# A row-wise softmax with relative-position bias: the last row of the first chunk in 16 small transfers on ScalarE's queue

## The chip, the cores and the metric

The kernel runs on one core of a Trainium2 chip. The metric is the device time of one execution in microseconds, lower is better. A core has VectorE (DVE), ScalarE (ACT), GpSimd (POOL), TensorE (PE, not used here) and SyncE (SP), and 16 DMA engines that move data between the chip's memory (HBM) and the on-chip memory of 128 partitions. DMAs are issued by SP and ACT, each on a queue of its own; in the profile SP's is q1 and ACT's is q10. The 16 engines serve both queues.

## The reference

```python
B, H, S, max_rel = 2, 8, 2112, 16
rel = pos[:, None] - pos[None, :]
rel_clipped = np.clip(rel, -max_rel, max_rel) + max_rel
logits = logits + rel_bias[:, rel_clipped][None]
logits = logits - logits.max(axis=-1, keepdims=True)
exp = np.exp(logits)
return exp / exp.sum(axis=-1, keepdims=True)
```

The logits are 2 x 8 x 2112 x 2112 in float32, 285 MB; as much is written. The bias has 33 values per head, chosen by the clipped distance of row and column.

## The kernel before, in words

**Tiles.** A row of scores has S = 2112 elements, 8448 B. W = 33 consecutive rows go to one partition, and 64 such groups make one head; the 128 partitions hold two heads. A round k (K = 4 of them, L202) handles two heads of both batch entries. Within a round the 33 rows of a partition are cut into chunks of 6, 5, 6, 5, 6, 5 rows (SIZES), for b = 0 and b = 1, so a round has NT = 12 chunks, and a row of a partition lies contiguous in memory, as do a chunk's rows. There are four buffers X[0] to X[3] (NBUF); chunk m uses X[m % 4], with a semaphore `ld` for its load and `st` for its store.

**Bias strip.** The tile F holds the bias as a strip of 2112 + 32 values per partition; row i of a partition adds the strip shifted by i. F is built from rel_bias once per round by `strip(k)` (L143 to L158) on DVE. Before the first round, rel_bias itself is loaded into the start of F by one DMA on ACT's queue (L107), over four partitions, after DVE has zeroed that part (L105); DVE waits for it at L133 (semaphore `rb`), spreads it by a shuffle (L134) and copies it into place (L140).

**Compute of a chunk.** `add(m)` on DVE takes the load's semaphore and, for each row, adds the strip, negates and finds the minimum (L173). `exps(m)` on ACT takes each row as it comes and does the exponential with its sum (L181). `scale(m)` on DVE takes all of a chunk's exponentials, forms the reciprocals (L189) and scales the first DV = 3 rows (L193); `scale_rest(m)` on ACT scales the others (L198). DVE's order in a round is strip, then add(0), scale(0), add(1), scale(1) and so on; ACT's is exps(0), scale_rest(0), exps(1) and so on.

**Transfers.** SP issues all loads (L88) and stores (L96). First the four loads of chunks 0 to 3, one after another without a wait; then store(0); then for each next chunk n: store n, wait until store n - 1 has landed, and load chunk n + 3 into the buffer so freed (`turn`, L215 to L219). `take` (L83) waits for a semaphore to reach a value and takes that off again. The last chunk's store is cut into two, its first three rows and the rest.

A transfer over 128 partitions with n rows of chunk m has this shape of addresses, one contiguous run per partition:

```python
ap=[[W * S, P], [1, n * S]]
```

Of the kernel before, what the change touches and what calls it, by code (L numbers as in the profile page):

```python
# [15 lines left out]
def kernel(  # L16
# [6 lines left out]
    nc = tc.nc  # L23
    P = 128
    B, H, S, S2 = logits.shape
    assert S == S2
    MR = 16
    W = 2 * MR + 1
# [5 lines left out]
    NBUF = 4  # L34
    SIZES = [6, 5, 6, 5, 6, 5]
# [8 lines left out]
    X = [io.tile([P, R * S], FP32, tag=f"X{b}", name=f"X{b}") for b in range(NBUF)]  # L44
# [11 lines left out]
    def view(t, offset, dims):  # L56
        return bass.AP(tensor=t.tensor, offset=t.offset + offset, ap=[[list(t.ap[0])[0], P]] + dims)

    def rows(t, k, m, s0, n):

        b, j, r = CH[m]
        return bass.AP(
            tensor=t.tensor,
            offset=t.offset + (b * H * S + j + s0) * S + k * (2 * S * S),
            ap=[[W * S, P], [1, n * S]],
        )

    with tc.tile_critical(no_gpsimd_drain=True):  # L68
        ld = [nc.alloc_semaphore(f"ld{b}") for b in range(NBUF)]
        st = [nc.alloc_semaphore(f"st{b}") for b in range(NBUF)]  # L70
        added = nc.alloc_semaphore("added")
        expd = nc.alloc_semaphore("expd")
# [13 lines left out]
        def load(k, m):  # L86
            b, r = m % NBUF, CH[m][2]
            nc.sync.dma_start(out=X[b][:, 0 : r * S], in_=rows(logits, k, m, 0, r)).then_inc(ld[b], 16)  # L88
# [8 lines left out]
                out=rows(out, k, m, s0, n), in_=X[b][:, s0 * S : (s0 + n) * S]  # L97
            ).then_inc(st[b], 16)

        for m in range(NBUF):  # L100
            load(0, m)

        Q = 32
        step = list(F.ap[0])[0]
# [3 lines left out]
            out=bass.AP(tensor=F.tensor, offset=F.offset, ap=[[Q * step, P // Q], [1, H * W]]),  # L108
            in_=bass.AP(tensor=rel_bias.tensor, offset=rel_bias.offset, ap=[[0, P // Q], [1, H * W]]),
# [7 lines left out]
        v = nc.vector  # L117
        done = [0]

        def then(ins):  # L120
            done[0] += 1
            ins.then_inc(dve, 1)

        def settle():
            take(v, dve, done[0])
            done[0] = 0
# [9 lines left out]
        for h in range(2):  # L136
            p = slice(h * NB, (h + 1) * NB)
            src = bass.AP(tensor=F.tensor, offset=F[p].offset + h * W,
                          ap=[[list(F.ap[0])[0], NB], [2 * W, K], [1, W]])
# [3 lines left out]
        def strip(k):  # L143

            then(v.tensor_copy(out=rbK[:, :], in_=rbP[:, bass.ds(k, 1), :]))  # L145
            settle()
            low, high = rbK[:, W - 1 : W], rbK[:, 0:1]
            blocks = view(F, MR, [[W, NB], [1, W]])
            then(v.tensor_tensor(out=blocks, in0=view(eq, 0, [[1, NB], [0, W]]),  # L149
                                 in1=view(rbK, W - 1, [[0, NB], [-1, W]]), op=ALU.mult))  # L150
            then(v.tensor_scalar(out=rest, in0=lt, scalar1=low, scalar2=None, op0=ALU.mult))  # L151
            then(v.tensor_copy(out=F[:, 0:MR], in_=low.to_broadcast([P, MR])))  # L152
            then(v.tensor_copy(out=F[:, FW - MR : FW], in_=high.to_broadcast([P, MR])))  # L153
            settle()
            then(v.scalar_tensor_tensor(out=rest, in0=gt, scalar=high, in1=rest, op0=ALU.mult, op1=ALU.add))  # L155
            settle()
            then(v.tensor_tensor(out=blocks, in0=blocks, in1=view(rest, 0, [[1, NB], [0, W]]), op=ALU.add))  # L157
            settle()  # L158
# [10 lines left out]
        def add(m):  # L169
            take(v, ld[m % NBUF], 16)  # L170
            j, r = CH[m][1:]
            for i in range(r):
                v.tensor_tensor_reduce(  # L173
                    out=row(m, i), in0=row(m, i), in1=F[:, W - 1 - j - i : W - 1 - j - i + S],
                    scale=-1.0, scalar=BIG, op0=ALU.add, op1=ALU.min, accum_out=col(nmax, m, i),
                ).then_inc(added, 1)
# [9 lines left out]
        def scale(m):  # L186
            r = CH[m][2]
            take(v, expd, r)
            v.reciprocal(out=col(rec, m, 0, r), in_=col(tot, m, 0, r)).then_inc(inv, 1)  # L189
            v.wait_ge(inv, 1).then_inc(inv, -1)  # L190
            v.sem_inc(invA, 1)
            for i in range(DV):
                v.tensor_scalar_mul(out=row(m, i), in0=row(m, i), scalar1=col(rec, m, i)).then_inc(scaled, 1)  # L193
# [7 lines left out]

        with nc.Fori(0, K, 1, engines=[ENG.DVE]) as k:  # L202
            strip(k)
            for m in range(NT):
                add(m)
                scale(m)
# [54 lines left out]
```

## Time and profile before

| what | value |
|---|---|
| time, median of 3 runs | 1329.12 us (1329.1 to 1329.44) |
| the profiled execution's own time | 1329.3 us |
| its span, from first to last instruction | 1327.5 us |
| moved | 571.00 MB, half read and half written |
| DVE, ACT busy | 819.7 us, 808.8 us |

In a line of the timeline the numbers are the start and the length in us, then the engine, the line of the code and the operation; "SPq" and "ACTq" are the queues of instructions of SP and ACT that issue DMAs, and an "x4" merges four issues into the stretch from the first's start to the last's end. A bracket gives the idle time of the engine before the instruction and what ended it. "DMA to landing" is the time from an issue to the completion of its transfer.

### The profile page before, as it was taken

To read this page: it belongs to the slowest core of one execution; us is meant where nothing else is said; L and a number is where in the kernel's file an instruction comes from. 1 tells how busy PE (TensorE), PEld (TensorE's weight loads), DVE (VectorE), ACT (ScalarE), POOL (GpSimd) and SP (SyncE) were. 2 spreads that over 40 slices of the span, in tenths; PEclk is the share of its full clock that TensorE was granted. 3 is DMA by queue.
4 is the path that set the end of the run, shared out by engine and by line. 5 is a ranking of instruction groups with operands and counts; after the bars stand their busy time and mean duration, and the time that the engine had idled before them with its cause. 6 is when DMAs were issued, how large, how long until landed. Compare 5 with 4: busy or idle time off the path is not lost. (4 is left out here: it accounts for less than half of the span.)

```text
span 1327.5 us, 2383 instructions
## 1 busy us (share of the span) xinstructions
DVE 819.7 (62%) x756; ACT 808.8 (61%) x652; POOL 0.6 (0%) x6
## 2 busy tenths in 40 slices
DVE  6875665558655566556866466664686547665572
ACT  3885575655756557555676566764667646675472
POOL 0000000000000000000000000000000000000000
DMA  9999999999999999999999999999999999999998
GB/s 407 427 424 425 430 433 429 432 431 433 434 430 438 423 439 431 432 432 433 438 436 429 433 430 435 433 430 441 427 439 428 435 431 437 434 436 427 436 427 376
DMA packets 13981, 571.00 MB, mean 430 GB/s; under 512 B 1556, under 2 KB 1560, under 8 KB 1560
## 3 DMA queue, kind: packets, MB, share of 16 engines
q1 hardware_dynamic: 13968, 570.96, 99.8%
q14 instruction: 5, 0.04, 0.0%
q10 hardware_dynamic: 8, 0.00, 0.0%
HBM read 285.48 MB, written 285.47 MB: 430 GB/s over the span
## 5 line engine op out<-in xcount | busy, mean ns | idle before, releaser
L173 DVE CUSTOM_DVE_ANT_0 X<-X,F 128x2112 f32<-128x2112 f32 x264 | 605.5, 2354 | 346.8 <-DVEq L83 346.8
L181 ACT ACTIVATE X<-X,nmax 128x2112 f32<-128x2112 f32 x264 | 542.2, 2054 | 411.5 <-ACTq L83 385.7
L198 ACT ACTIVATE X<-X,rec 128x2112 f32<-128x2112 f32 x120 | 238.7, 2046 | 29.0 <-ACTq L83 29.0
L193 DVE TENSOR_SCALAR X<-X,rec 128x2112 f32<-128x2112 f32 x144 | 181.4, 1316 | 11.6 <-DVEq L190 11.6
L189 DVE RECIPROCAL rec<-tot 128x6 f32<-128x6 f32 (+1 forms) x48 | 9.1, 190 | 116.1 <-DVEq L83 116.1
L181 ACT ACTIVATION_READ_ACCUMULATOR X<-X,nmax 128x1 f32 x264 | 49.3, 187 | 0.0
L181 ACT ACT_TABLE_LOAD x4 | 5.1, 1283 | 55.8 <-ACTq L83 55.8
L173 DVE DVE_READ_ACCUMULATOR2_ANT nmax<- 128x1 f32 x264 | 21.7, 82 | 0.0
L157 DVE TENSOR_TENSOR F<-F,rest 128x2112 f32<-128x2112 f32 x4 | 9.4, 2358 | 0.6
L149 DVE TENSOR_TENSOR F<-Z,rbK 128x2112 f32<-128x2112 f32 x4 | 9.4, 2358 | 0.6
L134 DVE LOAD_MASK_SELECT F<-F x1 | 0.0, 14 | 7.1 <-DMA F<-in_rel_bias_dram 7.1
L155 DVE SCALAR_TENSOR_TENSOR rest<-Z,rbK,rest 128x64 f32<-128x64 f32 x4 | 1.1, 284 | 0.6 <-DVEq L83 0.2
L151 DVE TENSOR_SCALAR rest<-Z,rbK 128x64 f32<-128x64 f32 x4 | 1.1, 275 | 0.0
L105 DVE MEMSET F<- 128x264 f32 x1 | 0.3, 278 | 1.1 <-SPq L68 1.1
L145 DVE COPY rbK<-rbP 128x33 f32 x4 | 0.7, 178 | 0.3 <-DVEq L83 0.3
L153 DVE COPY F<-rbK 128x16 f32<-128x16 f32 x4 | 0.7, 168 | 0.0
L152 DVE COPY F<-rbK 128x16 f32<-128x16 f32 x4 | 0.7, 166 | 0.0
L132 DVE TENSOR_SCALAR Z<-F 128x64 f32<-128x64 f32 x3 | 0.5, 223 | 0.1
L140 DVE COPY rbP<-F 64x132 f32<-64x132 f32 x2 | 0.4, 224 | 0.2
L134 DVE STREAM_SHUFFLE F<-F 128x264 f32<-128x264 f32 x1 | 0.4, 443 | 0.0
L112 POOL IOTA F<- 64x64 f32 x2 | 0.4, 179 | 0.7 <-PEq L256 0.6
L245 POOL MEMSET const-bfloat16-1.0<- 128x1 bf16 x1 | 0.1, 103 | 0.0
(3 smaller groups left out, 0.3 us busy)
## 6 DMA issues: line engine op xcount, KB each, us to landing
X<-in_logits_dram SPq DMA_DIRECT2D x24, 6336.0 KB, 39.7
out_dram<-X SPq DMA_DIRECT2D x24, 6336.0 KB, 46.9
X<-in_logits_dram SPq DMA_DIRECT2D x24, 5280.0 KB, 42.2
out_dram<-X SPq DMA_DIRECT2D x23, 5280.0 KB, 48.6
out_dram<-X SPq DMA_DIRECT2D x1, 3168.0 KB, 16.5
out_dram<-X SPq DMA_DIRECT2D x1, 2112.0 KB, 21.1
F<-in_rel_bias_dram ACTq DMA_DIRECT2D x1, 4.1 KB
```

Of the source, the lines that this page charges most:

```text
L145: then(v.tensor_copy(out=rbK[:, :], in_=rbP[:, bass.ds(k, 1), :]))
L149: then(v.tensor_tensor(out=blocks, in0=view(eq, 0, [[1, NB], [0, W]]), in1=view(rbK, W - 1, [[0, NB], [-1, W]]), op=ALU.mult))
L151: then(v.tensor_scalar(out=rest, in0=lt, scalar1=low, scalar2=None, op0=ALU.mult))
L152: then(v.tensor_copy(out=F[:, 0:MR], in_=low.to_broadcast([P, MR])))
L153: then(v.tensor_copy(out=F[:, FW - MR : FW], in_=high.to_broadcast([P, MR])))
L155: then(v.scalar_tensor_tensor(out=rest, in0=gt, scalar=high, in1=rest, op0=ALU.mult, op1=ALU.add))
L157: then(v.tensor_tensor(out=blocks, in0=blocks, in1=view(rest, 0, [[1, NB], [0, W]]), op=ALU.add))
L173: v.tensor_tensor_reduce(out=row(m, i), in0=row(m, i), in1=F[:, W - 1 - j - i : W - 1 - j - i + S], scale=-1.0, scalar=BIG, op0=ALU.add, o ...
L181: nc.scalar.activation(out=row(m, i), in_=row(m, i), func=ACTF.Exp, scale=-1.0, bias=col(nmax, m, i), accum_out=col(tot, m, i),).then_inc( ...
L189: v.reciprocal(out=col(rec, m, 0, r), in_=col(tot, m, 0, r)).then_inc(inv, 1)
L193: v.tensor_scalar_mul(out=row(m, i), in0=row(m, i), scalar1=col(rec, m, i)).then_inc(scaled, 1)
L198: nc.scalar.activation(out=row(m, i), in_=row(m, i), func=ACTF.Copy, scale=col(rec, m, i),).then_inc(scaledA, 1)
```

## The change

The first transfer of the program loads five of chunk 0's six rows per partition, in place of six. The sixth row (r0 = 5) of all 128 partitions comes by 16 further transfers on ACT's queue, each over some of the partitions in steps of G = 8: for g from 0 to 7 the partitions g, g + 8, ..., in all 15 - g of them (15, 14, ... 8 partitions), and then for g from 7 down to 0 the remaining g + 1 of each group (8, 7, ... 1 partitions). Each moves one row of 8448 B per partition. They stand in ACT's program ahead of the load of rel_bias, and need no wait. All of them count on a new semaphore `lr`, 16 for each transfer; DVE waits for the full 256 after strip(k) and ahead of add(0), in each round. The semaphore isn't taken down, so from the second round on it stands at 256. Loads 1 to 3, and chunk 0 of all later rounds, are as before.

```diff
+        lr = nc.alloc_semaphore("lr")
...
-        for m in range(NBUF):
+        G = 8
+        N0 = P // G
+        r0 = SIZES[0] - 1
+        nc.sync.dma_start(out=X[0][:, 0 : r0 * S], in_=rows(logits, 0, 0, 0, r0)).then_inc(ld[0], 16)
+        for m in range(1, NBUF):
             load(0, m)
+
+        def last_row(g, i0, n):
+            p0 = g + G * i0
+            x, d = X[0], rows(logits, 0, 0, r0, 1)
+            step = list(x.ap[0])[0]
+            nc.scalar.dma_start(
+                out=bass.AP(tensor=x.tensor, offset=x.offset + p0 * step + r0 * S, ap=[[G * step, n], [1, S]]),
+                in_=bass.AP(tensor=d.tensor, offset=d.offset + p0 * W * S, ap=[[G * W * S, n], [1, S]]),
+            ).then_inc(lr, 16)
+
+        for g in range(G):
+            last_row(g, 0, N0 - 1 - g)
+        for g in reversed(range(G)):
+            last_row(g, N0 - 1 - g, g + 1)
...
         with nc.Fori(0, K, 1, engines=[ENG.DVE]) as k:
             strip(k)
+            v.wait_ge(lr, 2 * G * 16)
             for m in range(NT):
                 add(m)
                 scale(m)
```

## The prediction
> **What bounds the kernel now.** I read the engines' busy shares first, then the DMA lines, then the windows and the first 80 us of the timeline. From the page:
>
> ```profile
> span 1327.5 us, 2383 instructions
> ...
> DVE 819.7 (62%) x756; ACT 808.8 (61%) x652; POOL 0.6 (0%) x6
> ...
> DMA packets 13981, 571.00 MB, mean 430 GB/s; under 512 B 1556, under 2 KB 1560, under 8 KB 1560
> ...
> q1 hardware_dynamic: 13968, 570.96, 99.8%
> q10 hardware_dynamic: 8, 0.00, 0.0%
> ...
> X<-in_logits_dram SPq DMA_DIRECT2D x24, 6336.0 KB, 39.7
> ```
>
> No compute engine is above 62%, while SP's queue (q1) alone keeps the 16 DMA engines occupied for 99.8% of the span. The windows after the start-up and of the tail:
>
> ```profile
> 60.00:1307.00 1247.00, 776.48 (x709) 773.95 (x624) 0.00 (x0) 1.00 1.00 433
> 1307.00:1327.50 20.50, 0.00 (x0) 0.00 (x0) 0.00 (x0) 1.00 0.78 338
> ```
>
> The columns after the length are the busy time of DVE, ACT and POOL, the granted clock, the DMA share and GB/s. In the middle the share is 1.00, so **the kernel is a stream of 571 MB**. A change moves the end only if it makes the DMA engines idle, or if the last engine to finish does so earlier. At the tail the share is 0.78: 0.22 x 20.5 = 4.5 us of mean idle, which holds the spread between the engines and the last landing.
>
> How full the stream is at the start decides this change:
>
> ```profile
> 0.97 1.88 SPq L88 DMA_DIRECT2D X<-in_logits_dram  x4
> ...
> 1.39 1.10 ACTq L107 DMA_DIRECT2D F<-in_rel_bias_dram  x1
> ...
> 9.08 0.01 DVE L134 LOAD_MASK_SELECT F<-F  x1 [7.10 <-DMA F<-in_rel_bias_dram]
> ...
> 14.10 2.36 DVE L157 TENSOR_TENSOR F<-F,rest 128x2112 f32<-128x2112 f32 x1
> 18.60 2.36 DVE L173 CUSTOM_DVE_ANT_0 X<-X,F 128x2112 f32<-128x2112 f32 x1 [2.15 <-DVEq L83]
> ```
> ```profile
> 41.38 16.61 SPq L96 DMA_DIRECT2D out_dram<-X  x2
> 75.06 0.36 SPq L88 DMA_DIRECT2D X<-in_logits_dram  x1
> ```
> ```profile
> 57.63 0.36 SPq L96 DMA_DIRECT2D out_dram<-X  x1
> ```
>
> Read them as a chain. The bias table is in at 9.08; the strip F is built from it and ends at 14.10 + 2.36 = 16.46; the first add starts at 18.60, held 2.15 us by chunk 0's load; the first store is issued at 41.38 and the second at 57.63. The landing times, of the four first loads, of the first load alone, and of the first store:
>
> ```profile
> L88 SPq DMA_DIRECT2D X<-in_logits_dram x4: 380/424/512, 1.0 to 2.3; - x4
> ...
> DMA to landing us min/median/max: 17.4/36.8/57.8
> ```
> ```profile
> DMA to landing us min/median/max: 33.5/33.5/33.5
> ```
>
> The last of the four was issued at 2.3 and landed 57.8 us later, at 60.1. Until then the engines have work whatever the compute does; store 0, in the queue since 41.38, follows without a gap and lands at 41.38 + 33.5 = 74.9. So **store 0 has slack**: a load of its size alone in the queue landed after 17.4 us, hence a store 0 issued at 74.9 - 17.4 = 57.5 would still land at 74.9. Each us after 57.5 is a us of idle DMA, and since nothing later in the span has idle time to give back, a us on the end.
>
> **The change part by part.** *Moved data.* 6336 KB are 6.488 MB; at 430 GB/s that is 15.1 us for six rows per partition, so one row of one partition (8448 B) takes one of 16 engines 15.1 / (8 x 6) = 0.314 us. A partition's packet takes 1.57 us with five rows and 1.89 us with six. The bytes stay the same. If the first partition of each small transfer goes to one and the same engine, that engine carries 16 of the 128 rows and the last engine none, in place of 8 each: 8 x 0.314 = 2.5 us more on one, 2.5 less on the other.
>
> *Order on ScalarE's queue.* The 16 new issues stand ahead of the rel_bias load (L107) in that queue. An issue takes between 0.34-0.5 us (SP's) and 1.10 us (L107's own), so L107 is issued between 1.39 + 16 x 0.34 = 6.8 and 1.39 + 17.6 = 19.0. ACT's first compute waits for F anyway, so the issue time costs nothing by itself. What counts is that the rel_bias packets now lie behind the last-row packets in the same DMA queue, q10; before, they had q10 to themselves.
>
> *How fast q10 drains beside q1.* The trace shows no such backlog, only this row pair: 4.1 KB whose issue ended at 1.39 + 1.10 = 2.49 are usable at 9.08, 6.6 us later, though they move in nothing. q10 had 8 packets for 4 partitions: four data and four completions (q1 likewise: 97 transfers x (128 + 16) = 13968). 6.6 us is about 3.5 q1 packets of 1.89 us: one or two under way, then the data, one more q1 packet, then the completion. I therefore take it that **an engine alternates, one packet of q1, one of q10**, and that a transfer needs two turns of q10 on each engine that it uses. The other end is free passage, with every q10 packet served on arrival.
>
> [...]
>
> *Which engine.* The engine that is in all 16 transfers has 16 data packets and 16 completions in q10, 32 turns; spread evenly it would be 8 and 8, 16 turns. No row shows which. I take the fixed start, because the simplest rule that gives all 97 large transfers exactly 8 rows and one completion per engine is a fixed one; the even spread stays as the other end. [...]
>
> *The sum.* On the busiest engine q1 holds 8 + 1 packets for each of the four first loads: 36 turns. rel_bias needs turns 33 and 34, plus up to two for packets under way: practically the end of the initial loads. That engine has 2.5 us more to do than before, so it ends them at 60.1 + 2.5 = 62.6, and rel_bias is in between 62.6 - 2 x 1.57 = 59.5 and 62.6: 61.0. From rel_bias to store 0 took 41.38 - 9.08 = 32.3, of which about 2.0 was the wait for chunk 0 (the 2.15 less some 0.15 of hand-over), gone now, because chunk 0 has long landed: 30.3. Store 0 is issued at 61.0 + 30.3 = 91.3, in place of at most 57.5: **33.8 us of idle DMA**. Then one bubble: store 1 is issued 57.63 - 41.38 = 16.25 after store 0, whose data lasts 15.1, and the next load must wait for store 0's landing: 1.15 us with nothing queued. After that load 4 and store 2 are queued in time (27 us of queue per chunk against 16 to 22 of compute), and the stream is full again. Total +35.0 on the profiled execution's 1329.3 (1.8 above its span, 0.2 above the median of 1329.12): **1364.3**.
>
> *The added wait.* `lr` at 256 stands on DVE behind strip and ahead of the first add; everything in the loop queues behind it, and ACT and SP behind that. The last-row packets land a turn or two before rel_bias, so it passes at once; with rel_bias early it alone would hold the first add to nearly 57, and only the 7.4 us of strip (9.08 to 16.46) would be hidden. The repeats in later rounds find 256 standing: nothing. Some 128 more completions of 4 B are 8 per engine; I price them at nothing on the stream, as 1.00 of share with 433 GB/s holds q1's own. If a row alone costs double, the busiest engine is 5 us later: 1369.
>
> **Rivals.** *1. One turn per transfer, or an even spread: 16 or 17 turns.* Five-row load 0 lands 2.5 us earlier than 0.97 + 17.4 = 18.4, at 15.9, plus nine interleaved rows of 0.314, 18.7 at turn 9; eight more turns of 1.57 + 0.31 give 33.8, one under way 35.4. Store 0 at 65.7, 8.2 late, with the bubble **1338.7**. For it: nothing forces the completion to a turn of its own. Against: 6.6 us for one row and its completion.
>
> *2. The other side: faster by the skew.* If q10 passes freely, rel_bias is in 7.7 us (1.39 to 9.08) after an issue at 6.8 to 19.0, that is 14.5 to 26.7, and store 0 goes at 57.0 at the latest. **The point is 57.5 - 30.3 = 27.2**: rel_bias in before that, no idle at all. Then only the skew is left, and if the last engine to finish is the one that carries no last row, the end comes up to 2.5 us sooner: **1326.8**, the 4.5 us of the tail allowing it. Against: the 7.10 us wait for 4 KB.
>
> [...]
>
> *4. The change does not do what it says:* the odd partition counts put all 128 rows on one engine: 120 x 0.314 = 37.7 us more there, rel_bias at 98, store 0 at 128: **1401**. Against: 8 packets for rel_bias's four partitions, one engine each as I read it.
>
> **How the numbers follow.** Forecast 0.70; rival 1 0.14; rival 2 0.05; rival 3 0.08; rival 4 0.03. The range takes the forecast with its bounds (rel_bias 59.5 to 62.6, double row cost, a few us of further bubbles: to 1372) and reaches down to rival 1: 1336 to 1372, 0.84. A change of over 0.2%, 2.7 us, can be told from none. Forecast, rivals 1 and 4 and a hundredth of the rest are slower: 0.88. Of rivals 2 and 3, 0.09 lies within 0.2% and 0.03 is faster.
>
> **What would show it.** DVE's wait at L134 for rel_bias grows from 7.10 to about 59 us; the first add starts near 68 with no wait of its own beyond it; store 0 is issued near 91; the DMA share falls to nothing from about 60 to 92, has a short dip near 108, and is 1.00 after; the tail is unchanged. L107's issue start gives the price of an issue. A wait at L134 below 18 us would disprove the alternation; one near 26 to 28 would mean one turn per transfer; a full DMA row with a later end would mean that the skew, not the start, sets the time.

## The result and the profile after

| | before | with the change |
|---|---|---|
| median of 6 runs each | 1329.57 us (1329.1 to 1329.95) | 1372.55 us (1371.81 to 1373.19) |
| span of the profiled execution | 1327.5 us | 1371.0 us |

The ratio is 1.0323, with a 95% interval of 1.031 to 1.0337: 43 us slower. The forecast was 1364.3, in a range of 1336 to 1372; the direction and the mechanism hold, the size is 8 us short and the measured time lies just above the range. The profile says where it is short.

From the page, the GB/s in 40 slices and the DMA lines:

```profile
GB/s 360 334 47 417 418 425 428 430 430 430 437 434 425 437 430 433 432 435 436 434 428 439 430 437 435 433 434 434 428 438 431 437 435 432 435 434 427 439 432 373
...
q1 hardware_dynamic: 13968, 569.87, 96.9%
q10 hardware_dynamic: 264, 1.09, 0.2%
```

The third slice, 69 to 103 us, has 47 GB/s: the stream has a hole, and nothing like it elsewhere. q10 now holds 264 packets: the 8 of rel_bias, 128 rows and 128 completions (the page counts 1684 packets under 512 B, 1556 before), so each small transfer has one completion for each of its rows, which fits one engine for each partition, down to the single one. No view lists the packets of one engine: an engine's turns and its share of the rows are the author's estimates from these counts, here and below.

The start of the timeline (start, length, engine, line, operation), and the first store and next load on SP's queue:

```profile
0.92 12.26 ACTq L112 DMA_DIRECT2D X<-in_logits_dram  x16
...
13.22 0.55 ACTq L126 DMA_DIRECT2D F<-in_rel_bias_dram  x1
67.79 0.01 DVE L153 LOAD_MASK_SELECT F<-F  x1 [65.81 <-DMA F<-in_rel_bias_dram]
...
75.50 2.36 DVE L192 CUSTOM_DVE_ANT_0 X<-X,F 128x2112 f32<-128x2112 f32 x1 [0.34 <-DVEq L84]
```
```profile
98.28 16.61 SPq L97 DMA_DIRECT2D out_dram<-X  x2
115.38 0.36 SPq L89 DMA_DIRECT2D X<-in_logits_dram  x1
```

rel_bias is issued at 13.22 and usable at 67.79, against 9.08 before. The first add follows F at once (0.34 us of idle), so neither `lr` nor the load holds it. From rel_bias to store 0 it takes 98.28 - 67.79 = 30.5 us; 30.3 had been worked out.

Windows of the same trace (length; busy DVE, ACT, POOL; clock; DMA share; GB/s), and the landing times of loads 1 to 3 and of store 0:

```profile
0.00:60.00 60.00, 0.76 (x4) 0.00 (x0) 0.56 (x6) 1.00 0.98 368
...
60.00:67.00 7.00, 0.00 (x0) 0.00 (x0) 0.00 (x0) 1.00 0.59 249
67.00:99.00 32.00, 27.18 (x30) 20.19 (x17) 0.00 (x0) 1.00 0.00 0
99.00:113.00 14.00, 11.34 (x12) 12.87 (x12) 0.00 (x0) 1.00 1.08 463
113.00:118.00 5.00, 5.00 (x4) 2.52 (x2) 0.00 (x0) 1.00 0.64 272
118.00:1350.00 1232.00, 775.19 (x709) 773.06 (x624) 0.00 (x0) 1.00 1.00 432
```
```profile
DMA to landing us min/median/max: 34.3/52.4/65.6
```
```profile
DMA to landing us min/median/max: 16.9/16.9/16.9
```

The engines run empty between 60 and 67, stand for 32 us while DVE and ACT work on chunk 0, stream store 0, have a short hole before store 1, and are full from then on at the old pace. The hole is 0.36 x 5 = 1.8 us at most; the window ahead of it reads 1.08, more than full, so the edge between the two isn't exact, and over both together 1.8 - 0.08 x 14 = 0.7 us are missing. Store 0 lands at 98.28 + 16.9 = 115.2, in place of 74.9: 40.3 us. With the hole that is 41.0 to 42.1 of the 43.5 us between the spans. The other 1.4 to 2.5 us are less than one GB/s of 433 over 1232 us makes (2.8 us), and stay unassigned.

The same loss can be told by the rate. In the first 60 us the share is 0.98 and the stream moves 368 GB/s, where the kernel before moved 410 at the same share (its line is shown with the single transfer below): 42 x 60 / 433 = 5.8 us are lost while the engines count as busy. From 60 to 99 they stand idle for 0.41 x 7 + 32 = 34.9 us, close to the 33.8 us of idle DMA in the forecast. So most of what the forecast lacks is not idle time but the slower stream ahead of it.

### The profile page after: what moved, and what is told of

It reads as the page before. It is cut to its first block, busy times and chain, and to the rows that moved or that the text cites. A ratio compares the mean times of both kernels' runs of the same rounds, so it can differ in the third digit from the quotient of the medians.

```text
span 1371.0 us, 2399 instructions
## 1 busy us (share of the span) xinstructions
DVE 819.5 (60%) x756; ACT 808.6 (59%) x652; POOL 0.6 (0%) x6
## 2 busy tenths in 40 slices
DMA packets 14237, 571.00 MB, mean 416 GB/s; under 512 B 1684, under 2 KB 1688, under 8 KB 1688
## 3 DMA queue, kind: packets, MB, share of 16 engines
q1 hardware_dynamic: 13968, 569.87, 96.9%
## 6 DMA issues: line engine op xcount, KB each, us to landing
X<-in_logits_dram SPq DMA_DIRECT2D x25, 5280.0 KB, 42.1
```

## The experiments

The theory: the chain from rel_bias to store 0 starts late because q10 gives one packet per packet of q1, and the hole is the time that store 0 comes too late. Its rivals: only the place of rel_bias in the queue matters, only the uneven share, or a fixed price per packet.

**rel_bias issued first.** The two loops of last_row move behind the load of rel_bias:

```diff
-        for g in range(G):
-            last_row(g, 0, N0 - 1 - g)
-        for g in reversed(range(G)):
-            last_row(g, N0 - 1 - g, g + 1)
...
         ).then_inc(rb, 16)
+        for g in range(G):
+            last_row(g, 0, N0 - 1 - g)
+        for g in reversed(range(G)):
+            last_row(g, N0 - 1 - g, g + 1)
```

> The rel_bias load is issued on ScalarE's queue ahead of the 16 last-row transfers; all else as in the changed kernel. Theory (an engine alternates one packet of q1 with one of q10, so whatever is in q10 drains only as the first four loads do): rel_bias is in near 9 us, strip is done near 17, but the wait for lr holds the first add until about 67, since the busiest engine still has 34 turns of q10. Store 0 at about 67.5 + 22.8 = 90, some 8 us earlier than in the changed kernel (98.28): about 1364 us. Rival (the last rows are in early, and only the place of rel_bias behind them in the queue costs): first add near 20, store 0 near 43, about 1330 us.

Measured: 1365.97 us, ratio 1.027 (1.024 to 1.03). The timeline:

```profile
8.62 0.01 DVE L153 LOAD_MASK_SELECT F<-F  x1 [6.64 <-DMA F<-in_rel_bias_dram]
```
```profile
67.68 2.36 DVE L192 CUSTOM_DVE_ANT_0 X<-X,F 128x2112 f32<-128x2112 f32 x1 [51.69 <-DVEq L84]
...
90.46 16.61 SPq L97 DMA_DIRECT2D out_dram<-X  x2
```

rel_bias is back at 8.62, and the first add now waits 51.69 us at the semaphore and starts at 67.68. The rival falls: rel_bias at its old time leaves 36 of the 43 us in place. Two waits ended at nearly the same time, and removing one uncovers the other. What is gained is the building of the strip, which now comes ahead of the wait: store 0 goes at 90.46 in place of 98.28.

**And the wait for lr only ahead of the sixth row.**

```diff
+                if m == 0 and i == r0:
+                    v.wait_ge(lr, 2 * G * 16)
                 v.tensor_tensor_reduce(
```

> As with rel_bias first, and the wait for lr stands ahead of the sixth row's add of chunk 0 instead of ahead of the first row's. Theory: five rows are added and exponentiated early; the sixth waits to about 67; from the end of the last add to store 0 the kernel before took 41.38 - 32.36 = 9.0, so store 0 is at about 67 + 2.4 + 9.0 = 78.5 and the time about 20 us under the changed kernel's, 1353 us. Rival (the landing of the last rows doesn't hold the start): no difference to the kernel before, 1330 us.

Measured: 1353.75 us, ratio 1.0178 (1.0148 to 1.0208). The sixth row's add and the first store:

```profile
67.52 2.36 DVE L194 CUSTOM_DVE_ANT_0 X<-X,F 128x2112 f32<-128x2112 f32 x1 [36.87 <-DMA X<-in_logits_dram]
...
78.81 16.61 SPq L97 DMA_DIRECT2D out_dram<-X  x2
```

It starts at 67.52 as before, but five rows are through, and store 0 goes at 78.81. In the three kernels store 0 is issued at 98.28, 90.46 and 78.81, and the times are 1372.55, 1365.97 and 1353.75: the loss follows the length of the chain between the last packet of q10 and store 0. The time at which that packet lands hardly changes with what waits for it.

**The last row in one transfer over 128 partitions**, on the same queue ahead of rel_bias:

```diff
...
+        nc.scalar.dma_start(out=X[0][:, r0 * S : (r0 + 1) * S], in_=rows(logits, 0, 0, r0, 1)).then_inc(lr, 16)
...
+            v.wait_ge(lr, 16)
```

> The last row in one transfer over 128 partitions on ScalarE's queue, ahead of rel_bias: each engine has 8 rows and one completion in q10, 11 turns until rel_bias is in. Theory: in the changed kernel's trace a row in q10 beside a q1 packet took some 0.45 us more than the two alone; 8 rows at 2.3 us a turn and three turns more put rel_bias at 25 to 27 us, store 0 at 56 to 57, just in time, so no idle DMA; the 8 x 0.45 = 3.6 us of slower transfers are lost on every engine: about 1333 us. If that extra is no loss of the stream: 1330 us. Rival (any split of the first load costs what the change cost): 1372 us.

Measured: 1330.3 against 1330.18 us, ratio 0.9999 (0.999 to 1.0008). The timeline, and the first 60 us as one window, here and in the kernel before:

```profile
19.99 0.01 DVE L150 LOAD_MASK_SELECT F<-F  x1 [18.01 <-DMA F<-in_rel_bias_dram]
...
50.49 16.60 SPq L97 DMA_DIRECT2D out_dram<-X  x2
```
```profile
0.00:60.00 60.00, 36.31 (x41) 28.46 (x25) 0.56 (x6) 1.00 0.97 410
```
```profile
0.00:60.00 60.00, 43.19 (x48) 34.82 (x29) 0.56 (x6) 1.00 0.98 410
```

rel_bias is 10.9 us later than before and store 0 9.1 us later, and it costs nothing, because 50.49 is still ahead of 57.5: the slack of the prediction covers it. Both come earlier than expected (19.99 against 25 to 27, 50.49 against 56 to 57). The expected extra of 0.45 us a row isn't there either: 410 GB/s in both, so the 128 rows beside the loads cost no throughput here. One transfer in place of the 16 is worth the whole 42 us (1330.3 against 1372.55).

**Eight transfers over 16 partitions** (every eighth), in the same place: by estimate an even share, half the turns.

```diff
...
+        for g in range(G):
+            last_row(g, 0, N0)
...
+            v.wait_ge(lr, G * 16)
```

> The last row in 8 transfers over 16 partitions each, on ScalarE's queue ahead of rel_bias: the same bytes, each engine 8 rows and 8 completions, 16 turns instead of up to 32. Theory (turns count): a row and its completion took 3.9 us on an engine in the changed kernel's trace, so rel_bias is in after about 2.3 + 8 x 3.9 + 2 more turns = 37 to 38 us, store 0 near 68, about 1341 us. Rival (the uneven share of the engines is what costs): an even share brings all of it back, 1330 us. Rival (many transfers on the queue cost by their issue): half the issues, half the loss, 1351 us.

Measured: 1341.42 us, ratio 1.0085 (1.0056 to 1.0115).

```profile
35.23 0.01 DVE L151 LOAD_MASK_SELECT F<-F  x1 [33.25 <-DMA F<-in_rel_bias_dram]
...
65.72 16.61 SPq L97 DMA_DIRECT2D out_dram<-X  x2
```

rel_bias comes at 35.23, store 0 8.2 us after the 57.5. The bytes are those of the one transfer, but q10 has 264 packets in place of 152: spread evenly over 16 engines that is eight completions each in place of one, 16 turns ahead of rel_bias in place of 9, and rel_bias is 35.23 - 19.99 = 15.2 us later, by this estimate 2.2 us for each of the seven. So the delay goes with the number of turns; an even share alone doesn't bring all of the loss back, and half the issues don't leave half of it (1351).

**Shorter packets in q1.** The first attempt gave the first four loads addresses of three dimensions, one run per row:

```diff
+                out=bass.AP(tensor=x.tensor, offset=x.offset, ap=[[list(x.ap[0])[0], P], [S, n], [1, S]]),
+                in_=bass.AP(tensor=d.tensor, offset=d.offset, ap=[[W * S, P], [S, n], [1, S]]),
```

> The changed kernel, but the first four loads on SyncE's queue have addresses with one run per row of 8448 B instead of one run per partition of five or six rows; all 16 transfers, the skew and the order stay. Theory (a turn of q10 waits for one packet of q1, so its price is the length of that packet): a turn falls from 1.6 to 1.9 us to about 0.3, 34 turns take some 16 to 24 us, rel_bias is in at 20 to 28 us, no idle DMA, 1330 to 1335 us. Rival (a packet of q10 costs a fixed latency of about 2 us beside a busy q1, whatever q1's packets are): rel_bias stays near 68 us, 1372 us.

Measured: 1372.41 us, which reads like the rival. But the page of that run has

```profile
q1 hardware_dynamic: 13968, 569.87, 96.9%
```

the same number of packets as before: adjoining rows still went as one run, and the run tests nothing. The second attempt issued each row as a transfer of its own:

```diff
...
+            for i in range(first[m]):
+                nc.sync.dma_start(out=X[m][:, i * S : (i + 1) * S], in_=rows(logits, 0, m, i, 1)).then_inc(
+                    lx[m] if i + 1 < first[m] else ld[m], 16)
...
+                if m < NBUF:
+                    v.wait_ge(lx[m], 16 * (first[m] - 1))
```

> The changed kernel, with the first four loads on SyncE's queue issued as 21 transfers of one row per partition each, so that q1's packets at the start really are 8448 B long; DVE also waits for these transfers ahead of chunks 0 to 3. In the run meant for this the packets of q1 had stayed as they were (13968 of them). Theory (a turn of q10 waits for one packet of q1): 34 turns at 0.3 to 0.6 us, rel_bias is in between 20 and 30 us, its issue at 13 us being the floor; store 0 at 50 to 60, hardly any idle DMA: 1330 to 1334 us. Rival (a packet in q10 costs a fixed 2 us beside a busy q1): rel_bias near 68 us, 1372 us.

Measured: 1336.37 us, ratio 1.0045 (1.0028 to 1.0061). The page and the timeline:

```profile
q1 hardware_dynamic: 16416, 569.88, 99.3%
```
```profile
27.55 0.01 DVE L156 LOAD_MASK_SELECT F<-F  x1 [25.57 <-DMA F<-in_rel_bias_dram]
```

With short packets in q1 and the same 16 transfers, rel_bias comes at 27.55 in place of 67.79. So the delay goes with the length of q1's packets, 8448 B here in place of 42240 or 50688, and a fixed price of 2 us (rel_bias near 68) falls. One thing changed besides: SP took 42.31 us to issue these 21 loads, so q1 may have held fewer of them at a time; the DMA share of 0.93 and 1.00 in the first two stretches of 20 us says that the engines still had work. The time is 2 us above the expected range. In those two stretches the stream moved 271 and 387 GB/s; such a loss of rate is the matter of the next runs.

**The 16 transfers on SP's queue**, between load 0 and load 1, so that rel_bias waits for none of them:

```diff
-            nc.scalar.dma_start(
+            nc.sync.dma_start(
...
+        for m in range(1, NBUF):
+            load(0, m)
```

> The 16 transfers stay, with the same uneven share, but on SyncE's queue between the first load and the other three; rel_bias is alone in ScalarE's queue as before. Theory: no alternation, rel_bias near 9 us; the last rows follow load 0 directly and are in by about 20 to 22 us; store 0 near 45, no idle DMA; what is left is the uneven share, 2.5 us at most either way: 1327 to 1332 us. Rival (the uneven share itself makes the loss): near 1372 us.

Measured: 1334.36 us, ratio 1.0031 (1.002 to 1.0042), above the expected 1327 to 1332. The uneven share isn't the loss of 43 us. But 4.2 us remain, more than the 2.5 of the share. The first three stretches of 20 us have 337, 372 and 428 GB/s, 379 in the mean, in place of 410: 31 x 60 / 433 = 4.3 us, all of it. So the rate falls here too, where the last rows stand in q1 itself and rel_bias, alone in q10, is in at 8.07.

**The 16 transfers for chunk 3's last row**, behind rel_bias on ScalarE's queue, so that their delay is hidden:

```diff
-        r0 = SIZES[0] - 1
+        r0 = SIZES[3] - 1
...
+                if m == 3:
+                    v.wait_ge(lr, 2 * G * 16)
```

> The same 16 uneven transfers on ScalarE's queue, but of the last row of chunk 3, which is needed only near 77 us, and behind rel_bias; the wait for lr stands ahead of chunk 3's first add. The alternation stays, its delay is hidden. Theory A (a row in q10 beside a q1 packet takes 0.45 us of engine time more than the two alone, and that is lost to the stream): the busiest engine loses 16 x 0.45 + 2.5 = 9.7 us, the mean 3.6: between 1333 and 1339 us. Theory B (the alternation delays q10 but loses no throughput): 1328 to 1332 us.

Measured: 1336.43 us, ratio 1.0045 (1.0031 to 1.0059): 6.3 us are lost without any idle DMA to speak of (a share of 0.98 in the first 60 us, as before the change, and 1.00 from there to 1310). That is inside theory A's range, but the 128 rows of the one transfer cost nothing, so it isn't a price of each row. To see whether the uneven share is their cause, the same with **8 even transfers**:

> Chunk 3's last row again on ScalarE's queue behind rel_bias, hidden until chunk 3 is due, but as 8 transfers over 16 partitions, so with an even share. With the 16 uneven transfers this cost 6.3 us against the kernel before. Theory S (the uneven share itself is lost: the busiest engine ends 2.5 us and its slower rows later): most of it goes, at most 8 x 0.3 = 2.4 us stay: 1330 to 1332.6 us. Rival (every transfer in q10 costs the stream by its presence): the same 128 completions, the same loss, 1336 us.

Measured: 1337.28 us, ratio 1.0056 (1.0042 to 1.007). Theory S falls on this queue: an even share loses no less. The first 60 us of the two, uneven and even:

```profile
0.00:60.00 60.00, 39.74 (x45) 33.52 (x28) 0.56 (x6) 1.00 0.98 364
```
```profile
0.00:60.00 60.00, 38.38 (x44) 32.17 (x27) 0.56 (x6) 1.00 0.98 362
```

The share is 0.98 as before, but the engines move 364 and 362 GB/s in place of 410. At 433 GB/s, 46 and 48 GB/s over 60 us are 6.4 and 6.7 us, against 6.3 and 7.2 us measured: nearly the whole loss. The engines were busy and slow. How much they slow is not a matter of the transfers' shape alone: the same eight transfers with chunk 0's row, above, had 372, 385 and 433 GB/s, at most 13 x 60 / 433 = 1.8 us of lost rate, and no run says why chunk 3's row costs more. On **SP's queue with 8 even transfers**:

> The last row on SyncE's queue between load 0 and load 1, as 8 transfers over 16 partitions instead of the 16 uneven ones (4.2 us over the kernel before). Theory S: the share of the engines is even, 2.5 us or more of the 4.2 go: 1330 to 1332 us. Rival (the small transfers in the stream and the later issue of the other loads are the loss): half of it goes at best, 1332 to 1334.4 us.

Measured: 1332.43 us, ratio 1.0018 (1.0009 to 1.0027). That lies in the rival's range, just above that of theory S: 1.8 of the 4.2 us go, and 2.4 stay, small but outside the interval around no change. Here the first 60 us have 348, 409 and 433 GB/s, 397 in the mean: 1.8 us.

**What makes a row slow.** One transfer over 128 partitions loses nothing, many small ones do. Two kernels test which partitions go together. The first has eight transfers over 16 neighbouring partitions each:

```diff
...
+            p0 = C * g
+            nc.scalar.dma_start(
+                out=X[0][p0 : p0 + C, r0 * S : (r0 + 1) * S],
...
```

> The 8 transfers over 16 partitions, but each over 16 neighbouring partitions instead of every eighth. Turns, bytes and completions per engine are the same as with every eighth (rel_bias in at 35.2, 1341.4 us). There a row with its completion took some 0.3 us longer than its row and the q1 packets alone. [...] Theory C (the extra is the price of a completion between rows): no difference, 1341 us.

Measured: 1348.62 us, ratio 1.0136 (1.0119 to 1.0153).

```profile
41.88 0.01 DVE L156 LOAD_MASK_SELECT F<-F  x1 [39.90 <-DMA F<-in_rel_bias_dram]
```

The other has 16 transfers, each over eight partitions in steps of 4:

```diff
...
+                    out=bass.AP(tensor=x.tensor, offset=x.offset + p0 * xs + r0 * S, ap=[[4 * xs, 8], [1, S]]),
...
```

> [...] Theory C (16 completions between rows cost 0.45 us each): rel_bias at 68 us, 1372.5 us.

Measured: 1370.34 us, ratio 1.0295 (1.0278 to 1.0312).

```profile
64.51 0.01 DVE L158 LOAD_MASK_SELECT F<-F  x1 [62.53 <-DMA F<-in_rel_bias_dram]
```
```profile
0.00:20.00 20.00, 0.76 (x4) 0.00 (x0) 0.56 (x6) 1.00 0.93 384
20.00:40.00 20.00, 0.00 (x0) 0.00 (x0) 0.00 (x0) 1.00 1.04 424
40.00:60.00 20.00, 0.00 (x0) 0.00 (x0) 0.00 (x0) 1.00 0.91 356
```

The same three windows of the changed kernel:

```profile
0.00:20.00 20.00, 0.76 (x4) 0.00 (x0) 0.56 (x6) 1.00 0.92 338
20.00:40.00 20.00, 0.00 (x0) 0.00 (x0) 0.00 (x0) 1.00 1.04 385
40.00:60.00 20.00, 0.00 (x0) 0.00 (x0) 0.00 (x0) 1.00 0.98 380
```

With equal bytes, as many transfers and as many packets (264 on q10 in both) and other partitions, neighbours are 6.65 us later than every eighth (41.88 against 35.23). The stream is slowed as well: the first two stretches of 20 us have 293 and 333 GB/s in place of 372 and 385. Steps of 4 are 3.3 us earlier than the changed kernel (64.51 against 67.79), with 46 and 39 GB/s more in the first two stretches of 20 us; there each transfer has eight partitions in place of 15 down to 1, which differs too, so this pair is the weaker one. Theory C, the price of a completion as the only extra, falls with both: it gave 1341 and 1372.5 us, and 1348.62 and 1370.34 were measured. So it matters which rows go together in a transfer. Why is not shown: with the partitions the source addresses change as well, no run held the one while it moved the other, and the eight transfers with chunk 3's row go to the same partitions as those with chunk 0's and lost more (6.7 us of rate against at most 1.8).

## Why the prediction was wrong

*The bound and the slack:* right. The stream's hole is most of the loss, and the 57.5 us are bracketed by the kernel with one transfer (store 0 at 50.49, no loss) and the one with eight (65.72, 11 us). The 33.8 us of idle DMA came out too (34.9), since rel_bias and the end of the initial loads were late together.

*Turns, one packet each, and a transfer's two turns per engine:* right as far as the times show it. It was read from one transfer of 4 KB, and the runs with fewer completions (rel_bias in at 19.99 and 35.23), shorter q1 packets (27.55) and another order (8.62) bear it out; no view lists the packets of one engine, so the order packet by packet stays an inference from these times. The rivals of one turn per transfer and of free passage put rel_bias at 35.4 us or earlier; it came at 67.79. No run bears out the 0.08 that the chances give to rival 3 either. The sign given for one turn per transfer, a wait near 26 to 28, doesn't fit that rival's own sum: 35.4 would be a wait of some 33.4.

*The same first engine:* an estimate that fits the delay; no view shows it. With an even spread rel_bias should be near the 35.23 of the eight transfers over 16 partitions; it came at 67.79.

*"Rel_bias is in between 59.5 and 62.6: 61.0":* **this is the step that failed**, by 6.8 us, and with it store 0 (91.3 forecast, 98.28 measured). The mis-sized term is the end of the initial loads, 60.1 + 2.5 = 62.6, to which rel_bias is tied. It priced a row in q10 at its 0.314 us and the q1 packets beside it at their usual length. The load that landed last came at 2.3 + 65.6 = 67.9, 7.8 us later than before, where 2.5 had been forecast for the busiest engine: the other 5.3 us fit the 5.8 us of rate lost at 368 in place of 410 GB/s. The bound of "a row alone costs double", 5 us, is of this size, but it stood in the range and not in the sum; with it the forecast would have been 1369. The kernel with steps of 4, with the same 264 packets in q10, takes 3.3 of the 6.8 back. The kernel with neighbours shows that the choice of partitions changes the rate (293 against 372 GB/s in the first 20 us); why the rate falls, and how the 5.3 us divide between the rows and the loads beside them, stays open.

*The bubble before store 1:* 1.15 forecast, 0.7 to 1.8 measured. *From rel_bias to store 0:* 30.3 forecast, 30.5 measured. *The issues:* 12.26 us for sixteen, inside the bounds, without effect of their own. *The added wait:* hidden behind rel_bias as forecast, and with rel_bias moved it held the first add to 67.68, where "nearly 57" was given: the same mis-sized term.

*The skew:* no run shows a gain from it. In the kernels where nothing else could hide one, the loss of rate in the first 60 us accounts for nearly the whole difference.

## What to carry to other kernels

Here the delay of rel_bias behind small transfers, beside a saturated queue, fits a wait of about one large packet of that queue for each row and each completion on an engine, however few the bytes: an estimate of 1.6 to 2.2 us a turn, from rel_bias's waits of 18.01 us over 11 turns (one transfer) and 39.90 over 18 (16 neighbours), its own two among them, beside packets of 1.57 and 1.89 us. In a kernel like this, count the turns, and put what the first computation needs ahead of everything else in its queue. Here a late start was free up to the point at which the first store had to enter the stream (50.49, no loss), and cost about microsecond for microsecond after it (store 0 8.2, 21.3 and 40.8 us after 57.5, for 11.3, 23.6 and 43.0 us); find that point from the last load's landing. Prefer one transfer over all 128 partitions: it cost nothing here (410 GB/s in the first 60 us, as before), while eight or 16 over a few partitions each slowed the stream (351 to 397 GB/s in the first 60 us), by an amount that differs between the kernels and for which no rule was found.

## What the runs showed that was not expected

- The stream lost 11% of its rate with its engines counted as busy: 364 GB/s at a share of 0.98 where 410 had the same share. The share alone didn't show this loss; GB/s beside it did.
- A second queue beside the first cost no throughput by itself: 410 GB/s with one transfer of 128 rows beside the loads, as without it.
- Addresses of three dimensions whose rows adjoin left q1 at 13968 packets; single-row transfers made them 16416. Only the packet count told that the first run had tested nothing.
- The issue of sixteen small transfers took 12.26 us, 0.77 us each, where SP issued four large loads in 1.88 us.
